# S4 of the split weights made by an addition on POOL instead of an accumulating transfer, and the first addition of a pair issued 8 units ahead

## The chip, the cores and the metric

The kernel runs on one core of one Trainium2 chip. The metric is the device time of one execution in microseconds (us). TensorE (PE) multiplies, VectorE (DVE) and ScalarE (ACT) prepare weights and activations, GpSimd (POOL) here issues transfers that add into on-chip memory (SBUF) and does a few elementwise operations, and SyncE (SP) issues the plain transfers.

## The reference

One layer of a hybrid encoder for 512 tokens with 1024 features, in float32: a half-step SwiGLU feed-forward network (ffn1), a mixer (a chunked state-space scan beside chunked attention), a second half-step feed-forward network (ffn2), and a final norm. The change touches the two feed-forward networks alone:

```python
def swiglu(h, w_gate, w_up, w_down):
    return (jax.nn.silu(h @ w_gate) * (h @ w_up)) @ w_down

x = x + 0.5 * swiglu(rms_norm(x, ffn1_norm[i]), ffn1_w_gate[i], ffn1_w_up[i], ffn1_w_down[i])
...
x = x + 0.5 * swiglu(rms_norm(x, ffn2_norm[i]), ffn2_w_gate[i], ffn2_w_up[i], ffn2_w_down[i])
```

The hidden width is 2816.

## The kernel before, in words

**Products.** Most of the feed-forward work uses Winograd's form of the 2x2 block product, with seven products in place of eight. For a piece d of the gate and up weights (128x1024 floats in each of its four blocks A11, A12, A21, A22) the stationary operands are P1: A11, P2: A12, P4: A22, P5: S1 = A21 + A22, P6: S2 = S1 + A11, P3: S4 = S2 + A12, and P7: A11 + A21. The sign conventions of the stored blocks make every one of these a sum. One product of one piece is a *unit* of 24 matmuls of 128x128 by 128x256 (line 541). The pieces of the first stretch of a network are multiplied plainly (units A11 to A22).

**The sums.** S1, S2 and S4 are built in place, in one tile per piece, `view(d)` (rows show it as `s`; there are four such places, in two wide tiles). A plain SP transfer brings A21 (line 324), and then POOL issues three transfers of 512 KB that add what they bring to what is there (`more`, line 327): A22 for P5, A11 for P6, A12 for P3. The single blocks g (P1), g2 (P2) and u2 (P4) come by SP into a `raw` tile (line 320, four buffers); P7's sum is added into g's buffer by POOL in the same way.

**Splits.** Float32 operands are multiplied as a rounded part and a remainder. `usplit` makes both for one weight tile: ACT casts (line 272) and DVE subtracts (line 274), into one of four rotating `xw` slots. `ws.get()` hands out the parts of the current unit and first makes the splits of the units up to 3 ahead. A transfer is issued when its unit is no more than its *lead* ahead: the numbers 14, 10, 6 and 5 in `product`. A step that reuses a tile waits for the split that last read it.

**Order.** Nothing is scheduled by a planner: each engine works through its instructions in the order in which the code emits them, and waits on semaphores. From the second Winograd piece on, a network runs P5(d), P1(d), P3(d-1), P4(d-1), P6(d), P2(d), P7(d). P6 and P7 are copied out of PSUM by ACT (lines 546 and 549); the two halves of the network's activations are then combined and split on DVE and ACT (lines 464, 465, 483 to 490, 522 to 570).

**The down projection** is cut into three blocks of pieces, named by tuples (n, a); the first two blocks are done in Winograd form in both networks (the third in ffn2 alone, with an order of its own, written out). A block takes its pieces in pairs: `down()` runs one product of both pieces, for token half t = 0 and then t = 1, 12 matmuls of 128x512 each (lines 142 to 144), and DVE adds each finished PSUM bank to the residual x at once (line 610). Products P1, P6, P7, P3 and P4 in turn go on accumulating in the banks of P1 (`X`) or in their own (`H`, `L`): P6 adds onto P1's banks, so its matmuls of a half wait until DVE has read P1's half. `DOWN` is the order of the products.

Of the kernel before, what the change touches and what calls it, by code (L numbers as in the profile page):

```python
# [12 lines left out]
ALU = mybir.AluOpType  # L13
# [24 lines left out]
def hybrid_block(ctx: ExitStack, tc, xT, xt, par, wgu1, wd1, ws1, win, wdt, wv, wo, rbt, wgu2, ws2, fin, out):  # L38
    nc = tc.nc
    V, S, G, T = nc.vector, nc.scalar, nc.gpsimd, nc.tensor  # L40
# [4 lines left out]
    def sb(tag, shape, dt=F32, bufs=1):  # L45
        uid[0] += 1
        return pool.tile(shape, dt, tag=tag, name=f"{tag}_{uid[0]}", bufs=bufs)
# [9 lines left out]
    def f(ap):  # L57
        return ap.bitcast(F32)
# [51 lines left out]
    class Stream:  # L110
# [16 lines left out]
        def get(self):  # L127
            i = self.used
            self.used += 1
            while self.done < min(len(self.jobs), i + 1 + self.look):  # L130
                job = self.jobs[self.done]
                job.move(0, True)
                job.parts = job.split()
                self.done += 1
            for n in range(self.done, min(len(self.jobs), i + 18)):
                self.jobs[n].move(n - i)
            return self.jobs[i].parts
# [95 lines left out]
    def wide_tile(g, dt=F32R):  # L233
        if g not in wide or wide[g][0] != dt:
            wide[g] = dt, sb(f"s{g}", [P, GROUPS[g], SEQ], dt)
        return wide[g][1]
# [30 lines left out]
    def usplit(src):  # L267

        i = turn[0] % 4
        turn[0] += 1  # L270
        hi = sb(f"xw{2 * i}", list(src.shape), F32R)
        S.copy(out=hi, in_=src)  # L272
        lo = sb(f"xw{2 * i + 1}", list(src.shape), F32R)
        V.tensor_tensor(out=lo, in0=src, in1=f(hi), op=ALU.subtract)  # L274
        return hi, lo

    DOWN = ("P5", "P1", "P2", "P6", "P7", "P3", "P4")

    def program(plain, by_tokens):


        if plain == 1:
            out = [("A11", 0), ("A21", 0), ("A12", 0), ("P1", 1), ("P5", 1), ("A22", 0), ("P6", 1), ("P2", 1), ("P7", 1)]
        else:
            out = [(a, d) for d in range(plain) for a in ("A11", "A21", "A12", "A22")]
            out += [(p, plain) for p in ("P5", "P1", "P6", "P2", "P7")]
        out = [("P", p, d) for p, d in out]
        for d in range(plain + 1, ND):  # L290
            out += [("P", p, e) for p, e in (("P5", d), ("P1", d), ("P3", d - 1), ("P4", d - 1), ("P6", d), ("P2", d),
                                             ("P7", d))]
            for n in range(2):
                if d == BLOCKS[n][1]:
                    out += [("S", n, p, (0, 1)) for p in DOWN]
        last = [("P", p, ND - 1) for p in ("P3", "P4")]
        if by_tokens == 3:
            return out + last + [("S", 2, p, (c,)) for c in range(2) for p in ("P5", "P1") + ("P2",) * (c == 0)] + [
                ("S", 2, "P6", (0, 1)), ("S", 2, "P2", (1,))] + [("S", 2, p, (0, 1)) for p in ("P7", "P3", "P4")]
        out += [("D", 2, 0, 0)] + last + [("D", 2, 1, 0), ("D", 2, 0, 1), ("D", 2, 1, 1)]  # L300
        return out + [("D", 2, o, c) for o in range(2, KD) for c in range(2)]

    def ffn_weights(wgu, plain, by_tokens, wst, wd=None):


        bufs, jobs, views = {}, {}, []

        def view(d):
            if d not in bufs:
                i = views.index(d)  # L310
                m = 2 if type(d) is int else min(2, BLOCKS[d[0]][1] - d[1])
                bufs[d] = wide_tile((40, 52)[i // 2 % 2], F32)[:, 2 * (i % 2):2 * (i % 2) + m]
                if type(d) is int:
                    bufs[d] = bufs[d].rearrange("p a (k c) -> p a k c", c=P)
            return bufs[d]

        def whole(key, src):
            def go():
                bufs[key] = sb("raw", list(src.shape), bufs=4)
                nc.sync.dma_start(out=bufs[key], in_=src)  # L320
            return go

        def first(d, src):
            return lambda: nc.sync.dma_start(out=view(d), in_=src)

        def more(get, src):
            return lambda: G.dma_start(out=get(), in_=src, accum_op=ALU.add)  # L327

        def product(p, d, A):

            sum_ = lambda: view(d)
            raw = {"P1": "g", "P2": "g2", "P4": "u2"}.get(p)
            if p[0] == "A":
                n = ("A11", "A12", "A21", "A22").index(p)
                j = Job(lambda: usplit(bufs[p, d]), (6, "raw", whole((p, d), A[n])))
            elif raw:
                j = Job(lambda: usplit(bufs[raw, d]), (6 if p == "P1" else 5, "raw",
                                                       whole((raw, d), A[("P1", "P2", "", "P4").index(p)])))
            elif p == "P5":
                views.append(d)  # L340
                before = jobs["P3", views[-5]] if len(views) > 4 else None
                j = Job(lambda: usplit(view(d)), (14, before, first(d, A[2])), (10, None, more(sum_, A[3])))
            elif p == "P6":
                j = Job(lambda: usplit(view(d)), (6, jobs["P5", d], more(sum_, A[0])))
            elif p == "P7":
                j = Job(lambda: usplit(bufs["g", d]), (6, jobs["P1", d], more(lambda: bufs["g", d], A[2])))
            else:
                j = Job(lambda: usplit(view(d)), (6, jobs["P6", d], more(sum_, A[1])))
            jobs[p, d] = j
            if p == "P7":  # L350
                jobs["P1", d].holds = j
            ws.jobs.append(j)

        for step in program(plain, by_tokens):
            if step[0] == "P":
                p, d = step[1:]
                product(p, d, wgu[d])
            elif step[0] == "S":
                n, p, pieces = step[1:]
                for a in [BLOCKS[n][0] + 2 * c for c in pieces]:  # L360
                    product(p, (n, a), [wst[i, :, a:min(a + 2, BLOCKS[n][1]), :] for i in range(4)])
            else:
                n, o, c = step[1:]
                if c == 0:
                    a, b = 2 * BLOCKS[n][0], 2 * BLOCKS[n][1]
                    ws.add(wd[o, :, a:b, :], b - a, P)
                    late = ws.jobs.pop() if (n, o) in ((2, 0), (2, 1)) else None
                    if late:
                        jobs["late", o] = late
                elif ("late", o) in jobs and n == 2:  # L370
                    ws.jobs.append(jobs["late", o])

    class XCombos:
# [40 lines left out]
        def split(self, d, src):  # L414
            S.copy(out=d[0], in_=src)
            V.tensor_tensor(out=d[1], in0=src, in1=f(d[0]), op=ALU.subtract)
# [25 lines left out]
    def ffn(xc, n_plain, early, by_tokens, rc, between, after):  # L442
# [174 lines left out]
        for step in program(n_plain, by_tokens):  # L617
            if step[0] == "S":
# [4 lines left out]
                down(*step[1:])  # L623
                past = step[1:3] == (1, DOWN[-1])
                continue
# [786 lines left out]
```

## Time and profile before

| what | value |
|---|---|
| median of 3 runs | 1033.45 us (1032.77 to 1034.1) |
| profiled execution, its own time | 1034.42 us |
| span of its instructions | 1032.6 us |
| mean granted TensorE clock | 0.995 of full speed |
| PE busy | 1007.5 us, 98% of the span |
| DVE, ACT, POOL busy | 809.0, 587.9, 162.2 us |

The profile is of one execution. Its own time is 1.82 us longer than the span, which begins with the first and ends with the last instruction, and 0.97 us above the median of the three timed runs. An engine's busy time is the sum over its instructions; a stall of PE shows as idle time before one of its rows, with what ended it.

### The profile page before, as it was taken

How to read it: one execution, taken by the hardware profiler on the slowest of the kernel's cores; microseconds unless marked ns; L12 is line 12 of the kernel's file. 1: busy time of each engine (PE TensorE's matmuls, PEld its weight loads, DVE VectorE, ACT ScalarE, POOL GpSimd, SP SyncE). 2: the span in 40 equal slices, each digit the busy share in tenths (PEclk: the TensorE clock that was granted, in tenths of full speed). 3: DMA queues.
4: the chain of work that ended last, by engine and by line, in shares of the span. 5: the costliest groups of instructions: out<-in, count | busy, mean ns of one | idle time of the engine just before them, and what ended most of it. 6: DMA issues, size and time to landing. Idle time of an engine off the chain costs nothing.

```text
span 1032.6 us, 16130 instructions
## 1 busy us (share of the span) xinstructions
PE 1007.5 (98%) x6154; PEld 888.0 (86%) x6154; DVE 809.0 (78%) x1351; ACT 587.9 (57%) x929; POOL 162.2 (16%) x185
## 2 busy tenths in 40 slices
PE   9999999999999999999999999999999999999985
PEld 7899889998998777777878778879998899989974
DVE  7878767886676697978867999797687678867876
ACT  7556445653564456646656876656654356534535
POOL 1111112121120013323201011101212121212110
PEclk9999999999999999999999999999999999999998
DMA  9979888996753322222232223765888989989672
GB/s 317 291 156 236 181 231 185 227 205 160 195 117 97 102 82 62 66 78 68 67 100 74 82 83 103 227 140 124 193 201 188 236 198 229 202 194 206 154 143 81
DMA packets 47933, 162.14 MB, mean 157 GB/s; under 512 B 5232, under 2 KB 6000, under 8 KB 47856
## 3 DMA queue, kind: packets, MB, share of 16 engines
q0 software_dynamic: 16704, 59.78, 33.2%
q1 hardware_dynamic: 28272, 95.43, 27.3%
q10 hardware_dynamic: 2880, 5.91, 1.7%
q8 instruction: 48, 0.79, 0.3%
q14 instruction: 29, 0.24, 0.1%
HBM read 159.00 MB, written 2.10 MB: 156 GB/s over the span
## 4 chain that ended last, share of the span: by engine, by line
PE 80%; DVE 9%; issue 4%; DMA 4%; ACT 3%; POOL 0%; SPq 0%; ACTq 0%; DVEq 0%; POOLq 0%
PE mm L541 19%; PE aux L541 14%; PE mm L142 10%; PE mm L143 10%; PE mm L144 10%; PE aux L144 3%; PE aux L143 3%; PE aux L142 3%; DMA raw<-wgu 2%; DVE fs L829 2%; DMA s<-wgu 1%; DVE wlo L86 1%; DVE xw L274 1%; ACT xw L272 1%; PE aux L953 1%
## 5 line engine op out<-in xcount | busy, mean ns | idle before, releaser
L541 PE MATMUL mm<-s,xw 128*128 128x256 f32 x1824 | 229.2, 283 | 2.8 <-ACT fu L549 2.8
L541 PEld LDWEIGHTS mm<-s,xw 128*128 128x128 f32 x1824 | 222.2, 191 | 4.1 <-ACT fu L549 3.4
L272 ACT CAST xw<-raw 128x1024 fp32r<-128x1024 f32 (+1 forms) x127 | 131.3, 1036 | 150.1 <-PE mm L541 54.6
L274 DVE TENSOR_TENSOR xw<-raw,xw 128x1024 fp32r<-128x1024 f32 (+1 forms) x127 | 152.7, 1203 | 63.8 <-ACT xw L272 63.7
L541 PE MATMUL aux<-s,xw 128*128 128x256 f32 x1368 | 174.1, 283 | 0.0
L541 PEld LDWEIGHTS aux<-s,xw 128*128 128x128 f32 x1368 | 168.8, 192 | 0.6
L272 ACT CAST xw<-s 128x1024 fp32r<-128x1024 f32 (+1 forms) x87 | 90.0, 1035 | 118.7 <-PE mm L144 40.1
L142 PE MATMUL mm<-xw,whi 128*128 128x512 f32 x364 | 149.6, 411 | 0.0
L274 DVE TENSOR_TENSOR xw<-s,xw 128x1024 fp32r<-128x1024 f32 (+1 forms) x87 | 104.7, 1203 | 56.9 <-ACT xw L272 55.0
L143 PE MATMUL mm<-xw,whi 128*128 128x512 f32 x364 | 144.8, 398 | 0.0
L144 PE MATMUL mm<-xw,wlo 128*128 128x512 f32 x364 | 144.4, 397 | 0.0
L84 ACT CAST whi<-raw 128x512 fp32r<-128x512 f32 (+1 forms) x104 | 62.2, 601 | 66.1 <-PE mm L143 46.9
L327 POOL DMA_DIRECT2D s<-wgu x57 | 51.4, 940 | 307.7 <-DMA s<-wgu 139.7
L86 DVE TENSOR_TENSOR wlo<-raw,whi 128x512 fp32r<-128x512 f32 (+1 forms) x104 | 74.3, 715 | 13.9 <-ACT whi L84 13.4
L142 PEld LDWEIGHTS mm<-xw,whi 128*128 128x128 f32 x364 | 68.9, 189 | 16.5 <-issue 2.2
L143 PEld LDWEIGHTS mm<-xw,whi 128*128 128x128 f32 x364 | 68.8, 189 | 16.2 <-issue 1.2
L144 PEld LDWEIGHTS mm<-xw,wlo 128*128 128x128 f32 x364 | 68.7, 189 | 16.2
L327 POOL DMA_DIRECT2D s<-ws x30 | 26.1, 869 | 167.9 <-DVE xw L274 70.2
L143 PE MATMUL aux<-xw,s 128*128 128x512 f32 x106 | 42.1, 397 | 2.9 <-DVE xw L274 2.9
L144 PE MATMUL aux<-xw,s 128*128 128x512 f32 x106 | 42.2, 398 | 0.0
L142 PE MATMUL aux<-xw,s 128*128 128x512 f32 x106 | 41.6, 394 | 0.0
L884 POOL TENSOR_TENSOR fu<-dt,tri 128x512 fp32r<-128x512 f32 x16 | 18.9, 1189 | 95.9 <-PE aux L935 45.5
(297 smaller groups left out, 1745.8 us busy)
## 6 DMA issues: line engine op xcount, KB each, us to landing
raw<-wgu SPq DMA_DIRECT2D x68, 512.0 KB, 5.6
s<-wgu POOLq DMA_DIRECT2D x57, 512.0 KB, 6.2
raw<-win SPq DMA_DIRECT2D x28, 512.0 KB, 3.5
s<-ws POOLq DMA_DIRECT2D x27, 512.0 KB, 5.7
raw<-ws SPq DMA_DIRECT2D x27, 512.0 KB, 4.6
s<-wgu SPq DMA_DIRECT2D x19, 512.0 KB, 5.4
raw<-wgu POOLq DMA_DIRECT2D x19, 512.0 KB, 5.8
raw<-wo SPq DMA_DIRECT2D x12, 512.0 KB, 3.7
```

Of the source, the lines that this page charges most:

```text
L84: S.copy(out=hi, in_=src)
L86: V.tensor_tensor(out=lo, in0=src, in1=f(hi), op=ALU.subtract)
L142: T.matmul(ps, lhsT=sh, rhs=mh, start=start, stop=False, skip_group_check=skip)
L143: T.matmul(ps, lhsT=sh, rhs=ml, start=False, stop=False, skip_group_check=skip)
L144: T.matmul(ps, lhsT=sl, rhs=mh, start=False, stop=stop, skip_group_check=skip)
L272: S.copy(out=hi, in_=src)
L274: V.tensor_tensor(out=lo, in0=src, in1=f(hi), op=ALU.subtract)
L327: return lambda: G.dma_start(out=get(), in_=src, accum_op=ALU.add)
L541: T.matmul(ps[:, j * HS:(j + 1) * HS], lhsT=sw[:, j, k], rhs=m, start=(p in ("P1", "P2", "P5") and j == 0 and k == 0 and n == 0), stop=(k ...
L829: V.scalar_tensor_tensor(out=y[:, d:SEQ], in0=u[:, 0:SEQ - d], scalar=cw(j), in1=y[:, d:SEQ], op0=ALU.mult, op1=ALU.add)
L884: G.tensor_tensor(out=r, in0=f(src[:, c, h0:h0 + 4]).unsqueeze(2).broadcast_to([P, 4, P]), in1=tri.unsqueeze(1).broadcast_to([P, 4, P]), o ...
L953: T.matmul(py[HD * (h % 2):HD * (h % 2) + HD, (h // 2) * P:(h // 2 + 1) * P], lhsT=xd[:, h * HD:(h + 1) * HD], rhs=st["m"][h // 4][:, (h % ...
```

## The change

For the pieces of the gate and up weights, and for blocks 0 and 1 of the down projection, P3's job has no transfer any more. The split of P2 first emits one POOL addition, `view(d) = view(d) + g2`, 128x1024 floats, and then its own cast and subtraction; A12 is the block g2, which P2 has in SBUF. The addition reads `view(d)` after P6's split has read it (S2 is in it until then) and reads the g2 buffer, so the next transfer into that buffer waits for it too. In `DOWN` P6 moves ahead of P2, so that S2 has been split when P2's split emits the addition. The lead of P5's second transfer goes from 10 to 8. Block 2 of ffn2's down projection keeps the transfer.

```diff
-    DOWN = ("P5", "P1", "P2", "P6", "P7", "P3", "P4")
+    DOWN = ("P5", "P1", "P6", "P2", "P7", "P3", "P4")
...
             sum_ = lambda: view(d)
+            here = type(d) is int or d[0] < 2
             raw = {"P1": "g", "P2": "g2", "P4": "u2"}.get(p)
...
+            elif p == "P2" and here:
+                def split():
+
+                    G.tensor_tensor(out=view(d), in0=view(d), in1=bufs[raw, d], op=ALU.add)
+                    return usplit(bufs[raw, d])
+                j = Job(split, (5, "raw", whole((raw, d), A[1])))
...
-                j = Job(lambda: usplit(view(d)), (14, before, first(d, A[2])), (10, None, more(sum_, A[3])))
+                j = Job(lambda: usplit(view(d)), (14, before, first(d, A[2])), (8, None, more(sum_, A[3])))
...
+            elif here:
+                j = Job(lambda: usplit(view(d)))
             else:
                 j = Job(lambda: usplit(view(d)), (6, jobs["P6", d], more(sum_, A[1])))
```

POOL's queue around the first down block and the first pieces after it, in ffn1. `s_45` and `s_113` are the two wide tiles of sums, `raw` the single blocks, `ws` the down weights and `wgu` the gate and up weights. Before (P6 of the block's first two pieces, P7, S4 of both, then the second additions of P5(4) on, with S4 of piece 5 the row 33):

```order
23 L327 DMA s_113_472<-ws 128x1024
24 L327 DMA s_45_150<-ws 128x1024
25 L327 DMA raw_1094<-ws 128x1024
26 L327 DMA raw_1132<-ws 128x1024
27 L327 DMA s_113_472<-ws 128x1024
28 L327 DMA s_45_150<-ws 128x1024
29 L327 DMA s_113_472<-wgu 128x1024
30 L327 DMA s_45_150<-wgu 128x1024 x2
31 L327 DMA raw_1394<-wgu 128x1024
32 L327 DMA s_113_472<-wgu 128x1024
33 L327 DMA s_45_150<-wgu 128x1024
```

And of the change, the same stretch:

```order
24 L327 DMA s_113_472<-ws 128x1024
25 L327 DMA s_45_150<-ws 128x1024
26 L327 DMA raw_1095<-ws 128x1024
27 L327 DMA raw_1133<-ws 128x1024
28 L340 TENSOR_TENSOR s_113_472<-s_113_472,raw_1244 128x1024
29 L340 TENSOR_TENSOR s_45_150<-s_45_150,raw_1276 128x1024
30 L327 DMA s_113_472<-wgu 128x1024
31 L327 DMA s_45_150<-wgu 128x1024 x2
32 L327 DMA raw_1395<-wgu 128x1024
33 L327 DMA s_113_472<-wgu 128x1024
34 L340 TENSOR_TENSOR s_45_150<-s_45_150,raw_1506 128x1024
```

Each S4 transfer is replaced in its place by an addition, and no other row of POOL moves: also the second addition of P5 stands where it stood, with a lead of 8 as with 10. There are 27 such rows in the kernel.

DVE's queue in the same down block: the residual additions (line 610 before, 619 after) of P5 (`aux`) and P1 (`mm`), and between them the remainders (line 274) of the next products. Before:

```order
144 L610 SCALAR_TENSOR_TENSOR x_62<-aux_1234,rcf_312,x_62 128x4x128
145 L274 TENSOR_TENSOR xw_220_1275<-raw_1201,xw_219_1273 128x1024
146 L610 SCALAR_TENSOR_TENSOR x_62<-aux_1235,rcf_312,x_62 128x4x128
147 L274 TENSOR_TENSOR xw_222_1280<-raw_1238,xw_221_1278 128x1024
148 L610 SCALAR_TENSOR_TENSOR x_62<-mm_1236,rcf_312,x_62 128x4x128
149 L274 TENSOR_TENSOR xw_226_1313<-s_113_472,xw_225_1311 128x1024
150 L610 SCALAR_TENSOR_TENSOR x_62<-mm_1237,rcf_312,x_62 128x4x128
151 L274 TENSOR_TENSOR xw_228_1319<-s_45_150,xw_227_1317 128x1024
152 L610 SCALAR_TENSOR_TENSOR x_62<-aux_1309,rcf_312,x_62 128x4x128
```

After:

```order
144 L619 SCALAR_TENSOR_TENSOR x_62<-aux_1235,rcf_312,x_62 128x4x128
145 L274 TENSOR_TENSOR xw_219_1274<-s_113_472,xw_218_1272 128x1024
146 L619 SCALAR_TENSOR_TENSOR x_62<-aux_1236,rcf_312,x_62 128x4x128
147 L274 TENSOR_TENSOR xw_222_1281<-s_45_150,xw_221_1279 128x1024
148 L619 SCALAR_TENSOR_TENSOR x_62<-mm_1237,rcf_312,x_62 128x4x128
149 L274 TENSOR_TENSOR xw_224_1313<-raw_1244,xw_223_1311 128x1024
150 L619 SCALAR_TENSOR_TENSOR x_62<-mm_1238,rcf_312,x_62 128x4x128
151 L274 TENSOR_TENSOR xw_226_1318<-raw_1276,xw_225_1316 128x1024
152 L619 SCALAR_TENSOR_TENSOR x_62<-mm_1237,rcf_312,x_62 128x4x128
```

P6's two remainders (from `s`) now stand at the places of P2's (from `raw`), and PE's 24 matmuls of P6 likewise ahead of P2's: the product that follows P1 is the one that goes on in P1's banks (`mm_1237`, `mm_1238`). This happens in four blocks, two in each network. On PE, ACT, DVE and SP nothing else changes its place.

## Rows read from the trace of the kernel before

**Rows 1.** The page's sections 1 and 3: busy time, transfer queues.

```profile
PE 1007.5 (98%) x6154; PEld 888.0 (86%) x6154; DVE 809.0 (78%) x1351; ACT 587.9 (57%) x929; POOL 162.2 (16%) x185
...
q0 software_dynamic: 16704, 59.78, 33.2%
```

**Rows 2.** What PE waited for: us in total, times, longest us.

```profile
PE mm L541 <- ACT fu L549: 2.8, 2, 2.1
```

**Rows 3.** Timeline of PE and ACT, ffn1 near P7(5): start, us, instruction [idle].

```profile
166.44 0.74 PE L541 MATMUL mm<-s,xw 128*128 128x256 f32 x4 [2.06 <-ACT fu L549]
...
162.47 1.05 ACT L272 CAST xw<-s 128x1024 fp32r<-128x1024 f32 x1 [4.55 <-DMA s<-wgu]
...
165.81 0.57 ACT L549 COPY fu<-mm 128x512 f32<-128x512 f32 x1
```

**Rows 4.** Timeline of PE and ACT, ffn2, the same place.

```profile
838.43 1.33 PE L541 MATMUL mm<-s,xw 128*128 128x256 f32 x9 [0.71 <-ACT fu L549]
...
834.46 1.05 ACT L272 CAST xw<-s 128x1024 fp32r<-128x1024 f32 x1 [3.20 <-DMA s<-wgu]
```

**Rows 5.** Line 327's transfers issued at 154.83, 827.74 and 165.18, in this order.

```profile
DMA to landing us min/median/max: 7.5/7.5/7.5
...
DMA to landing us min/median/max: 6.6/6.6/6.6
...
DMA to landing us min/median/max: 5.3/5.3/5.3
```

**Rows 6.** Timeline of SP's queue from 154: two transfers in one row.

```profile
155.17 3.58 SPq L320 DMA_DIRECT2D raw<-wgu  x2
```

**Rows 7.** Timeline of POOL in the mixer: additions of two inputs, 128x512.

```profile
400.56 1.04 POOL L884 TENSOR_TENSOR fh<-dt,tri 128x512 fp32r<-128x512 f32 x1
401.56 1.04 POOL L884 TENSOR_TENSOR fu<-dt,tri 128x512 fp32r<-128x512 f32 x1
...
413.09 1.48 POOL L884 TENSOR_TENSOR fh<-dt,tri 128x512 fp32r<-128x512 f32 x1
```

**Rows 8.** Timeline of DVE beside the last two of those.

```profile
413.60 0.27 DVE L958 TENSOR_TENSOR s<-s,aux 128x128 f32<-128x128 f32 x1
413.80 1.33 DVE L86 TENSOR_TENSOR wlo<-raw,whi 128x512 fp32r<-128x512 f32 x1
415.05 1.00 DVE L918 COPY dt<-s 128x4 f32<-128x4 f32 x1
```

**Rows 9.** Line 918 over the kernel: ns min/median/max, first and last start.

```profile
L918 DVE COPY dt<-s x12: 153/556/1017, 401.9 to 501.2; 128x4 f32<-128x4 f32 x12
```

**Rows 10.** Timeline of DVE, ACT and PE in ffn1 after P6(2)'s split.

```profile
51.71 1.23 DVE L274 TENSOR_TENSOR xw<-s,xw 128x1024 fp32r<-128x1024 f32 x1 [2.81 <-ACT xw L272]
...
53.45 0.68 DVE L465 TENSOR_TENSOR wlo<-fa,whi 128x512 fp32r<-128x512 f32 x1
...
59.82 0.58 ACT L546 COPY fa<-mm 128x512 f32<-128x512 f32 x1
...
60.45 1.81 PE L541 MATMUL mm<-s,xw 128*128 128x256 f32 x13
```

**Rows 11.** Timeline of DVE, PE and POOL in ffn2 after P6(1)'s split.

```profile
697.94 1.23 DVE L274 TENSOR_TENSOR xw<-s,xw 128x1024 fp32r<-128x1024 f32 x1 [0.59 <-ACT xw L272]
...
699.97 0.68 DVE L198 TENSOR_TENSOR s<-ident,rq_h 128x512 fp32r<-128x512 f32 x1
...
700.80 0.47 PE L205 MATMUL aux<-s,onesr 128*128 128x512 f32 x1 [0.18 <-DVE s L198]
...
699.58 0.86 POOL L327 DMA_DIRECT2D s<-wgu  x1 [9.96 <-DVE rq_r L171]
```

**Rows 12.** Timeline of DVE and PE in ffn1's first down block.

```profile
113.58 1.23 DVE L274 TENSOR_TENSOR xw<-raw,xw 128x1024 fp32r<-128x1024 f32 x1 [1.77 <-ACT xw L272]
...
120.27 0.74 DVE L610 SCALAR_TENSOR_TENSOR x<-mm,rcf,x 128x512 f32<-128x512 f32 x1
...
121.94 0.39 PE L142 MATMUL aux<-xw,s 128*128 128x512 f32 x1
```

## The prediction

> **What bounds the kernel now.** The page's first section says that PE is busy for 1007.5 of 1032.6 us [rows 1]. So a change to the weights' preparation can only give back PE's few stalls or make new ones, and the view to read next is that of PE's waits. Of its entries the two networks' weight path owns one that this change can reach: P7's first matmuls waiting for ACT's copy of P6 out of PSUM, 2.8 us in two places [rows 2]. The timeline shows both. In ffn1 PE stood still for 2.06 us ahead of P7(5), because the copy stood in ACT's queue behind the cast of P5(6), and that cast waited 4.55 us for a transfer; in ffn2 the same place cost 0.71 us, and there the cast waited 3.20 us [rows 3, 4]. Everywhere else in the Winograd stretches PE runs on from unit to unit, so transfers and splits are hidden there, and 27 fewer transfers on a queue that is 33.2% busy [rows 1] are worth nothing in themselves. What the change is worth is read at those two places, and at the places where the new additions stand in DVE's way.
>
> **What it removes: two late landings.** P5(6)'s second transfer was issued at 154.83 and took 7.5 us to land; its like in ffn2, issued at 827.74, took 6.6; one that runs alone takes 5.3 [rows 5]. What came between is in SP's queue: 0.34 us after the issue SP started a plain transfer of 512 KB [rows 6], P4(5)'s block into the buffer that P2(5)'s split had just given up. With the change that buffer is also read by the addition for piece 5, and that addition stands on POOL right behind P5(6)'s transfer (rows 33 and 34 of the order above). So SP's transfer can't start until POOL has issued, waited and added, some 3 us later, and P5(6)'s transfer goes first. At 5.3 us it lands 2.2 us earlier in ffn1 and 1.3 us earlier in ffn2. Both are more than the stall, so I take back all of both: **-2.06 and -0.71, together -2.8 us**. P4(5) is used two units after P5(6)'s split is cast and has the time to be late by 3 us. The bound on the other side is nothing at all, if the transfers still share the engines in a way that leaves P5(6) late; that is a rival below.
>
> **What it removes at no gain.** The other S4 transfers land unwaited for. The lead of 8 in place of 10 moves no row in any queue; nothing is counted for it. The stall in ffn2's last block, which keeps the transfer, stays as it is.
>
> **What one addition costs.** No row of before is a 128x1024 addition on POOL. The nearest are POOL's products of two inputs at 128x512 in the mixer: 1.04 us each with starts 1.00 apart when nothing disturbs them [rows 7]. Twice that is **a = 2.04 us**, and that is the value I take. Below it can't be under 1.04, the price of half the elements. Above, the same operation took 1.48 us in a stretch where DVE worked beside it [rows 7], so 2.96 for the double size; but that figure has DVE's turns in it, so I put the upper end midway, at 2.5.
>
> [...]
>
> **What it does to DVE.** POOL itself has the time (162 us busy [rows 1], and 27 additions bring 55). The question is whether DVE runs beside it. In the mixer it didn't, for operations that read SBUF: next to POOL's products a DVE copy of 4 elements took 1.00 us, where the shortest of the same line took 0.153, and a 128x512 remainder 1.33, while an operation with an operand in PSUM kept its 0.27 [rows 8, 9]. Each engine's instruction waited for the other's to end. So I take an addition as a time a in which DVE's remainders, splits and small operations stand still, and its readings of PSUM don't.
>
> The addition starts as soon as P6's remainder has ended on DVE, that is where DVE has just come back to its backlog. In most units there is slack for that: the splits run up to 3 units of 2.9 us ahead, and ACT's copy of P6 usually ends a good microsecond before P7. I found three kinds of places without it.
>
> *ffn1, piece 2.* P6(2)'s remainder ends at 52.94. The addition then holds DVE to about 55.05, and the activations' remainder that began at 53.45 begins there, 1.6 us late. It is the head of a chain through DVE (lines 483, 484) and two casts on ACT to ACT's copy of P1 at 59.82, which ended at 60.40, when PE began the next unit at 60.45 [rows 10]. There is no slack at the end and 0.1 to 0.2 on the way: **+1.4 us**.
>
> *ffn2, piece 1.* The remainder ends at 699.17. What follows on DVE is the chain of small operations that makes the norm's scale for PE: its last one ran from 699.97 and PE waited for it already, 0.18 us, before 700.80 [rows 11]. The addition falls into this chain (the transfer that it replaces was issued at 699.58 [rows 11]) and delays its end by all of a: **+2.0 us**. If DVE's row gets in first, the next one is caught, so I see no way past it short of the addition starting after 699.97.
>
> *The down blocks.* Here the swapped order matters. P6 now follows P1 and adds onto P1's banks, so PE needs DVE's reading of P1's second half when P6's second half begins. In the first block that is at 121.94, and without additions DVE would be done by 120.27 + 0.74 = 121.01 [rows 12]: 0.9 us to spare. With them DVE's row is: first remainder of P6 until 113.58 + 1.23 = 114.81; first addition from 114.90; second remainder of P6 until 116.13 + a; second addition from 116.22 + a; P2's remainder, which stands ahead of the reading, until 117.45 + 2a; the reading until 118.10 + 2a (rows of DVE overlap by 0.09). With a = 2.04 that is 122.18, a stall of 0.24; below a = 1.92 there is none. Four such blocks: **+1.0 us**, and this is the term that hangs most on a: 8 us for each us of it.
>
> **The sum.** -2.8 + 1.4 + 2.0 + 1.0 = +1.6 us. On the profiled execution's 1034.42 that is 1036.0; that execution was 0.97 us above the median, so against the median of 1033.45 the forecast is **1035.1 us**, 0.16% slower. A difference under 0.2%, 2.07 us here, is about what a measurement of this kernel can't tell from no change. The sum moves by 10 us for each us of a (two single places and eight times in the blocks), so a = 2.08 would already pass that limit, and with a = 1.92 the sum is +0.4.
>
> **The rivals.**
>
> *DVE is not held up.* If a contiguous addition leaves DVE its operands, all three losses vanish and the gain of 2.8 stays: 1030.7 us, faster. For it speaks that every unit has slack for one slower remainder, and that the slowed rows are all from one stretch of the mixer; against it that those rows show nearly whole waits, not a mild stretching. An addition as short as 1.04 us would hold DVE so little that the blocks cost nothing and the two places 0.4 and 1.0: 1032.1, no change that can be told. Chance of a faster result 0.2.
>
> *The addition is dearer.* With a from 2.1 to 2.5 the blocks decide: midway, at 2.3, each stalls by 0.76, and the sum is -2.8 + 1.7 + 2.3 + 3.0 = +4.2, which gives 1037.6; at 2.5 it is +6.2 and 1039.7. For it speaks that two separate inputs at full length have no row here; against it the 1.04. Chance 0.26. [...]
>
> *P5(6) stays late.* If its transfer doesn't come earlier (the late landing being due to something other than SP's transfer, or the addition finding its operands early enough to be issued first), the gain is gone and the sum is 1.4 + 2.0 + 1.0 = +4.4: 1037.9, slower. The issue at 155.17 right behind that at 154.83 speaks against it. Chance 0.12.
>
> **How the numbers follow.** My own case, losses and gain nearly level, has 0.42, and its own range is 1033.9 to 1035.5 (a from 1.92 to 2.08). The two slower rivals together have 0.38, the faster one 0.2. For eight times in ten the range reaches down to 1031.0, just above the case in which DVE isn't held at all, and up to 1038.2, past a = 2.3 and past a late P5(6), and short of a = 2.5.
>
> **What would show it.** In the trace of the changed kernel: additions of about 2.04 us at line 340, 27 of them. P7(5) without idle time ahead of it in both networks, P5(6)'s transfers landing in about 5.3 us, SP's transfer behind POOL's addition. A new wait of about 1.4 us of PE ahead of ffn1's unit near 60.4 (for ACT's line 555), one of 2 us at line 205 in ffn2 near 701, and waits at line 142 for DVE's line 619 of 0.2 us in each of four blocks. DVE's remainders beside an addition should show more than 1.23 us or begin as it ends. I am wrong if DVE's rows run at their usual length beside the additions, if the addition takes clearly other than 2 us, or if a unit that I took to have slack stalls.

## The result and the profile after

The changed kernel takes 1041.49 us (median of 8 runs, 1039.33 to 1042.15), the kernel before 1033.78 us on the same chip. The ratio is 1.0068, with a 95% interval of 1.0053 to 1.0084: some 7 us slower (the two medians stand 7.7 us apart), outside the forecast range of 1031.0 to 1038.2. The profiled execution took 1040.57 us, 6.15 us more than that of before, so it holds most of the difference.

The page's section 1 of the changed kernel, to be read beside [rows 1]:

```profile
PE 1010.3 (97%) x6154; PEld 888.5 (86%) x6154; DVE 848.5 (82%) x1351; ACT 590.0 (57%) x929; POOL 205.1 (20%) x185
...
q0 software_dynamic: 12816, 45.62, 25.2%
```

POOL's queue lost 14 MB, as intended, and POOL gained 43 us of work. The telling number is DVE's: 39.5 us more busy time with the same 1351 instructions. Part of that is waiting: a remainder of DVE that POOL held up is recorded as busy for 2.99 us (at 116.51, below), where one in [rows 10] took 1.23.

What PE waited for, to be read beside [rows 2] (us in total, times, longest us):

```profile
PE aux L143 <- DVE xw L274: 3.4, 1, 3.4
PE aux L205 <- DVE s L198: 2.4, 1, 2.4
PE mm L142 <- DVE x L619: 1.8, 4, 0.5
...
PE mm L550 <- ACT fa L555: 1.2, 1, 1.2
...
PE mm L550 <- ACT fu L558: 0.2, 1, 0.2
```

All three predicted waits are there and the one that was to go has gone (ACT's copy, line 558 now, from 2.8 us to 0.2). The first row is ffn2's last block, which the change leaves alone; it waited 2.9 us before.

The groups of POOL (busy us, mean ns of one):

```profile
L340 POOL TENSOR_TENSOR s<-s,raw 128x1024 f32<-128x1024 f32 x27 | 69.3, 2567 | 39.8 <-DVE xw L274 30.1 <-DVE rq_q L169 9.7
```

and line 340 by itself (ns min/median/max):

```profile
L340 POOL TENSOR_TENSOR s<-s,raw x27: 2377/2413/2793, 52.4 to 971.7; 128x1024 f32<-128x1024 f32 x27
```

An addition takes 2.41 us, and none took less than 2.377. I had put a = 2.04.

**Where the 6 us went.** Both kernels run the same 6154 matmuls in the same order but for the four swapped pairs, so the start of each can be compared with that of the same number before. The lag of the changed kernel grows and shrinks in few places: +1.2 us at ffn1's piece 2, +3.7 at ffn2's piece 1, 0.8 to 0.9 in each of the four blocks (3.4), -2.3 and -1.0 at the two P7(5), +0.5 near 206 us, +0.6 in ffn2's last block, and nothing in sum over the rest. Together 6.1. Each trace is of one execution: the first 58 us, ahead of the first loss, moved by -0.6 to +1.1 us from trace to trace, so a lag of half a us in one place is proof of nothing by itself.

At ffn2's piece 1 (timeline of DVE, POOL and PE, beside [rows 11]):

```profile
700.22 0.15 DVE L169 TENSOR_TENSOR rq_q<-rq_o 128x4 f32<-128x4 f32 x1
700.41 2.38 DVE L171 SCALAR_TENSOR_TENSOR rq_r<-rq_q,rq_v 128x4 f32<-128x4 f32 x1
702.82 0.16 DVE L173 SCALAR_TENSOR_TENSOR rq_o<-rq_r,rq_o 128x4 f32<-128x4 f32 x1
...
700.39 2.38 POOL L340 TENSOR_TENSOR s<-s,raw 128x1024 f32<-128x1024 f32 x1 [9.69 <-DVE rq_q L169]
...
704.14 0.77 PE L205 MATMUL aux<-s,onesr 128*128 128x512 f32 x1 [2.39 <-DVE s L198]
```

The addition started 0.02 us ahead of an operation on 4 elements, which then lasted as long as the addition, 2.38 us in place of 0.16. The norm's chain is late by all of it, and PE stood still for 2.39 us. What I had not counted follows (windows of PE: start and end, busy us, granted clock, DMA share):

```profile
700.00:704.00 4.00, 1.75 (x12) 1.00 0.00 0
704.00:705.00 1.00, 0.86 (x3) 0.57 0.00 0
705.00:706.00 1.00, 1.00 (x6) 0.50 0.00 0
706.00:707.00 1.00, 1.00 (x6) 0.50 0.46 33
707.00:708.00 1.00, 1.00 (x9) 0.73 0.55 197
708.00:709.00 1.00, 1.00 (x11) 1.00 0.72 295
```

Behind the idle time the granted clock was 0.50 of full speed for some 3 us; the lag grew by another 1.5 us there.

In ffn1's first block (timeline of DVE, POOL and PE, beside [rows 12]):

```profile
116.51 2.99 DVE L274 TENSOR_TENSOR xw<-s,xw 128x1024 fp32r<-128x1024 f32 x1
119.42 0.74 DVE L619 SCALAR_TENSOR_TENSOR x<-mm,rcf,x 128x512 f32<-128x512 f32 x1
120.26 2.82 DVE L274 TENSOR_TENSOR xw<-raw,xw 128x1024 fp32r<-128x1024 f32 x1
123.00 0.74 DVE L619 SCALAR_TENSOR_TENSOR x<-mm,rcf,x 128x512 f32<-128x512 f32 x1
...
116.02 2.40 POOL L340 TENSOR_TENSOR s<-s,raw 128x1024 f32<-128x1024 f32 x1 [2.03 <-DVE xw L274]
119.58 2.41 POOL L340 TENSOR_TENSOR s<-s,raw 128x1024 f32<-128x1024 f32 x1 [1.17 <-DVE xw L274]
...
123.80 0.50 PE L142 MATMUL mm<-xw,whi 128*128 128x512 f32 x1 [0.46 <-DVE x L619]
```

This is the row that the prediction laid out: remainder, addition, remainder, addition, P2's remainder, and only then the reading of P1's second bank, which PE waits for. The remainders start in time and end 1.1 us after the addition does (119.50 after 118.42, 123.08 after 121.99). The reading itself, an operand in PSUM, keeps its 0.74, also beside the second addition.

### The profile page after: what moved, and what is told of

Its sections match the earlier page's. It is cut to its first block, busy times and chain, and to the rows that moved or that the text cites. A ratio compares the mean times of both kernels' runs of the same rounds, so it can differ in the third digit from the quotient of the medians.

```text
span 1038.8 us, 16095 instructions
## 1 busy us (share of the span) xinstructions
PE 1010.3 (97%) x6154; PEld 888.5 (86%) x6154; DVE 848.5 (82%) x1351; ACT 590.0 (57%) x929; POOL 205.1 (20%) x185
## 4 chain that ended last, share of the span: by engine, by line
PE 81%; DVE 9%; ACT 3%; issue 3%; DMA 2%; POOL 0%; SPq 0%; ACTq 0%; POOLq 0%; DVEq 0%
PE mm L550 20%; PE aux L550 15%; PE mm L142 10%; PE mm L143 10%; PE mm L144 10%; PE aux L144 3%; PE aux L143 3%; PE aux L142 3%; DVE fs L838 2%; DVE xw L274 1%; DMA raw<-wgu 1%; ACT xw L272 1%; DVE wlo L86 1%; PE aux L962 1%; PE aux L753 1%
## 5 line engine op out<-in xcount | busy, mean ns | idle before, releaser
L274 DVE TENSOR_TENSOR xw<-raw,xw 128x1024 fp32r<-128x1024 f32 (+1 forms) x127 | 180.8, 1425 | 50.6 <-ACT xw L272 50.2
L274 DVE TENSOR_TENSOR xw<-s,xw 128x1024 fp32r<-128x1024 f32 (+1 forms) x87 | 111.7, 1284 | 44.4 <-ACT xw L272 44.0
L327 POOL DMA_DIRECT2D s<-wgu x38 | 33.4, 880 | 278.7 <-DMA s<-wgu 152.8
L340 POOL TENSOR_TENSOR s<-s,raw 128x1024 f32<-128x1024 f32 x27 | 69.3, 2567 | 39.8 <-DVE xw L274 30.1
L327 POOL DMA_DIRECT2D s<-ws x22 | 19.2, 874 | 123.8 <-DMA s<-ws 58.7
```

Of the source, the lines that this page charges most:

```text
L340: G.tensor_tensor(out=view(d), in0=view(d), in1=bufs[raw, d], op=ALU.add)
```

## The experiments

The diffs are against the changed kernel unless they say otherwise. The ratios are to the kernel before, with 95% intervals.

**1. Additions in the blocks alone** (`blocks_only`).

```diff
-            here = type(d) is int or d[0] < 2
+            here = type(d) is tuple and d[0] < 2
```

> Additions in the four down blocks alone, with the swapped order; all pieces of the gate and up weights keep the transfer. Theory (DVE stands still for 2.41 us per addition, and the reading of P1's second bank behind two of them makes PE wait): about +0.8 us per block over before, together +3.3 us (1.003), a wait of PE at line 142 for line 619 of about 0.5 us in each block; the late landings of P5(6) stay, 2.2 and 0.9 us. Rival (the blocks are harmless and the pieces carry the whole loss): no difference from before.

Measured: 1.0035 (1.0021 to 1.0049), +3.6 us. PE's waits for line 619 are the same four, 1.8 us in all; the lag grows by 0.8 to 0.9 us in each block. The theory holds and its rival falls: eight of 27 additions make half of the loss.

**2. Additions for the gate and up pieces alone** (`pieces_only`): `here = type(d) is int`, and the old `DOWN`.

> Additions for the gate and up pieces alone; the blocks keep transfer and old order. Theory: +1.2 (ffn1 piece 2), +3.7 (ffn2 piece 1, with the half clock behind the stall), +0.4 (piece 7), -3.1 (P5(6)): +2.2 us over before (1.002), 3.5 us under the whole change. Rival (blocks harmless): as slow as the whole change, +6 to +7 us.

Measured: 1.0035 (1.0020 to 1.0050), +3.6 us, a little over the 2.2 expected and with the interval's low end below it. The trace has the same waits (2.4 us at line 205, 1.0 for line 555) and none for line 619 in the blocks.

**3. The same without the first Winograd piece of each network** (`pieces_not_first`): `here = type(d) is int and d > plain`, and the old `DOWN`.

> As the pieces alone, but the first Winograd piece of each network (2 in ffn1, 1 in ffn2) keeps the transfer too. Theory: both single places are gone and the gain of 3.1 us at P5(6) stays: 2 to 3 us faster than before (0.9975). Rival (the gain at P5(6) comes with a loss that is spread over all units): no faster than before.

Measured: 0.9987 (0.9973 to 1.0002), 1.3 us faster, less than expected and not clear of no change, so the time alone doesn't rule the rival out. Against run 2 the medians differ by 4.7 us (1037.81 and 1033.07), which is about what the two places cost by the lags (1.2 + 3.7). The wait for line 555 is gone and that at line 205 is back at 0.2 us. The gain at P5(6) is in the lags (-2.3 and -1.0), and 0.8 us are lost again behind three remainders that were held up for longer than a unit's slack ("What was not foreseen", below).

**4. The addition on VectorE** (`on_dve`): `V.tensor_tensor` in place of `G.tensor_tensor`.

> The whole change with the addition on VectorE instead of POOL, at about 1.2 us. Theory (what costs is the time in which DVE does nothing else): the blocks lose nothing (two times 1.2 is under the 3.85 us of room), ffn2 piece 1 loses 1.2 us and perhaps the clock, ffn1 piece 2 nearly nothing, P5(6) is still relieved as SP's transfer waits 1.2 us more: between 2 us faster than before and no difference, and 6 us or more faster than the change. Rival (the loss comes from S4 made in SBUF or from the new order as such): as slow as the change.

Measured: 1.0017 (1.0002 to 1.0032), 1.8 us slower than before and 5 us faster than the change. The addition takes 1.22 us on DVE, and no block waits. Two things came out otherwise than I expected. Line 205 had no wait at all: the program put five more matmuls ahead of it on PE, so this place is no test (and PE's order is not only that in which the code is written, though the part on the kernel before says so). And P5(6) stayed late, with 3.6 us of waits ahead of the two P7(5):

```profile
PE mm L550 <- ACT fu L558: 3.6, 2, 1.9
```

The timeline of POOL and SP and, below it, the landing of line 327 issued at 155.62 say why:

```profile
155.62 0.86 POOL L327 DMA_DIRECT2D s<-wgu  x1 [9.45 <-DMA s<-wgu]
...
155.89 3.44 SPq L320 DMA_DIRECT2D raw<-wgu  x2
```

```profile
DMA to landing us min/median/max: 7.2/7.2/7.2
```

On DVE the addition is done before P2's remainder, so nothing holds SP's transfer back; it starts 0.27 us after POOL's and that one lands late, as in [rows 5, 6]. By the lags the two P7(5) cost 1.0 us each more than before, which comes to the loss of this run; at the first of them it is the clock, at 0.50 for some 3 us behind the wait.

This run also settles a rival that the prediction didn't name. Before, POOL issued the transfer of S4 of piece 5 right behind that of P5(6), two in one row:

```profile
154.83 1.77 POOL L327 DMA_DIRECT2D s<-wgu  x2 [9.24 <-DMA s<-wgu]
```

Here that second transfer is gone, SP's isn't held back, and P5(6)'s still takes 7.2 us. So it is SP's transfer that makes it late, and not that of S4.

**5. The swapped order and the lead alone** (`swap_lead_only`): `here = False`.

> No additions at all: only P6 ahead of P2 in the blocks, and the lead of 8. Theory: no difference from before (under 0.1%), since DVE would read P1's second bank 0.9 us before P6 needs it. Rival (the swapped order itself makes PE wait): +1 to +3 us, with waits at line 142 for line 619.

Measured: 1.0007 (0.9987 to 1.0028), no difference that can be told, and no wait for line 619. The order as such costs nothing in the blocks of this trace; it only takes away the slack that the additions then overdraw.

**6. One addition per network, for piece 5** (`piece5_only`): `here = d == 5`, and the old `DOWN`.

> One addition per network, for piece 5; everything else as before (the lead of 8 apart). Theory: SP's transfer now waits for that addition, P5(6)'s transfer lands in 5.1 to 5.4 us, and the stalls of 2.06 and 0.71 us ahead of P7(5) are gone: 2.8 to 3.1 us faster than before (0.997). Rival (the relief came from the other transfers that were removed): no difference.

Measured: 0.9976 (0.9958 to 0.9994), 2.5 us faster than before and the lowest ratio here, though its interval overlaps those of runs 3 and 9. Timeline of POOL, SP and PE, and below it the landing of line 327 issued at 154.91:

```profile
154.91 0.86 POOL L327 DMA_DIRECT2D s<-wgu  x1 [9.47 <-DMA s<-wgu]
155.47 2.74 POOL L340 TENSOR_TENSOR s<-s,raw 128x1024 f32<-128x1024 f32 x1
...
158.24 2.02 SPq L320 DMA_DIRECT2D raw<-wgu  x2
...
164.44 0.74 PE L550 MATMUL mm<-s,xw 128*128 128x256 f32 x4 [0.21 <-ACT fu L558]
```

```profile
DMA to landing us min/median/max: 5.5/5.5/5.5
```

SP's transfer waits until 158.24, P5(6)'s lands in 5.5 us where it took 7.5, and 2.06 us of PE's idle time become 0.21. With 25 of the 27 transfers back in place, the gain is all there: with run 4, where 27 transfers are gone and the gain is missing, it is a matter of who goes first, not of fewer bytes.

**7. Each addition in two halves** (`halves`): a loop over the two 128x512 parts of `view(d)` and g2.

> The whole change, but each addition as two of 128x512. Theory (a DVE instruction waits for the POOL instruction in progress to end, and they take turns): a half takes about 1.25 us; in ffn2 piece 1 the small operation waits 1.2 us, the next one for the second half, so the chain is about as late as before (2 to 2.4 us); in the blocks DVE's remainder gets in between the halves, with no or little gain in all: within 2 us of the change. Rival (DVE slips in freely at each boundary and is done after one half): waits at line 205 and in the blocks halved, 3 us or more faster than the change.

Measured: 1.0035 (1.0020 to 1.0051), 3.4 us faster than the change, more than the theory allowed. Here theory and rival were each right in a place. At ffn2's piece 1 (timeline of DVE and POOL):

```profile
699.50 1.29 DVE L171 SCALAR_TENSOR_TENSOR rq_r<-rq_q,rq_v 128x4 f32<-128x4 f32 x1
700.82 1.19 DVE L173 SCALAR_TENSOR_TENSOR rq_o<-rq_r,rq_o 128x4 f32<-128x4 f32 x1
702.05 0.17 DVE L194 CAST rq_h<-rq_o 128x4 fp32r<-128x4 f32 x1
...
699.48 2.52 POOL L342 TENSOR_TENSOR s<-s,raw 128x512 f32<-128x512 f32 x2 [9.65 <-DVE rq_q L169]
```

One small operation waits for each half, so PE still stood still for 2.3 us. In the blocks a remainder of DVE goes between the halves (in the first block remainders last 1.88, 1.63 and 1.65 us, where the change had 2.99 and 2.82), each is a whole instruction's worth of work, and the reading of P1's bank comes in time: no wait for it is left. In these places turns are taken by whole instructions. They aren't everywhere: some remainders waited for both halves, and the two longest, at 75.90 and 891.70 (4.25 and 4.34 us), cost 0.6 us each by the lags. With ffn2's piece 1 (3.7) and the gain at P5(6) (-3.1) that is 1.8 of this execution's 3.2 us of lag; another 1.1 arose in the first 10 us, ahead of any addition.

**8. What an addition costs by its inputs** (`price`), against the kernel before: five operations on POOL ahead of the attention stage.

```diff
+    G.tensor_tensor(out=pr, in0=x[:, 0:2], in1=x[:, 2:4], op=ALU.add)
+    G.tensor_tensor(out=pr[:, 0], in0=x[:, 0], in1=x[:, 2], op=ALU.add)
+    G.tensor_tensor(out=pr[:, 0], in0=x[:, 0], in1=x[:, 2], op=ALU.mult)
+    G.tensor_tensor(out=p4(pr[:, 0]), in0=wide4, in1=p4(x[:, 2]), op=ALU.add)
+    G.tensor_tensor(out=p4(pr[:, 0]), in0=wide4, in1=ones.unsqueeze(1).broadcast_to([P, 4, P]), op=ALU.mult)
```

> The kernel before with five extra POOL operations ahead of the attention stage, whose results nothing uses: an addition 128x1024, an addition 128x512, a product 128x512, an addition 128x512 with one input that repeats 4 values, a product 128x512 with both inputs repeated. Theory (the price depends on how the inputs are read): the first about 2.4 us, the full 128x512 ones about 1.2, the repeated ones about 1.04 as line 884. Rival (a price per element plus a fixed one, whatever the inputs): all 128x512 alike at 1.04 and the first at 2.4 for another reason.

The first and the last of the five are its lines 1244 and 1248. These two rows and, from run 7, that of line 342 (ns min/median/max):

```profile
L1244 POOL TENSOR_TENSOR raw<-x x1: 2392/2392/2392, 544.1 to 544.1; 128x1024 f32<-128x1024 f32 x1
...
L1248 POOL TENSOR_TENSOR raw<-x,ones x1: 1041/1041/1041, 555.2 to 555.2; 128x512 f32<-128x512 f32 x1
```

```profile
L342 POOL TENSOR_TENSOR s<-s,raw x54: 1259/1606/2292, 53.1 to 971.2; 128x512 f32<-128x512 f32 x54
```

With both inputs repeated from fewer values (line 884 reads its inputs like that, 4 values spread over 128 each and a 128x128 tile repeated) 512 elements take 1.04 us; with both read in full they take 1.26 at the least. The three operations between had DVE's turns in them (timeline of POOL: addition, product, addition with one repeated input; below it the instruction of DVE that each waited for):

```profile
548.38 1.80 POOL L1245 TENSOR_TENSOR raw<-x 128x512 f32<-128x512 f32 x1
...
550.26 1.63 POOL L1246 TENSOR_TENSOR raw<-x 128x512 f32<-128x512 f32 x1
...
553.76 1.31 POOL L1247 TENSOR_TENSOR raw<-x 128x512 f32<-128x512 f32 x1
```

```profile
548.34 0.69 DVE L86 TENSOR_TENSOR wlo<-raw,whi 128x512 fp32r<-128x512 f32 x1
...
549.55 1.19 DVE L86 TENSOR_TENSOR wlo<-raw,whi 128x512 fp32r<-128x512 f32 x1
...
553.48 0.69 DVE L86 TENSOR_TENSOR wlo<-raw,whi 128x512 fp32r<-128x512 f32 x1
```

Counted from the end of DVE's instruction, the addition and the product of full inputs both needed 1.15 us (550.18 - 549.03, 551.89 - 550.74), and the addition with one repeated input 0.90 (555.07 - 554.17), as line 884's products do before where DVE held them up (0.89 to 0.90 for the four that began from 411.57 to 415.99). The halves of run 7 need 1.15 there as well. So in these rows it is the repeated input that is cheaper and one is enough (shown by one row), and addition or product makes no difference.

**9. The change without its losses** (`harmless`): `here = d > plain if type(d) is int else d[0] < 2`, with two halves in the blocks alone.

> The change with its two kinds of loss taken out by their causes: the first Winograd piece of each network keeps the transfer, and each addition of the blocks is made as two of 128x512, so that DVE gets in between. 25 of the 27 transfers are still gone. Theory: no wait at line 205 beyond 0.2 us, none for line 555, none in the blocks, and the 3 us at P5(6) are gained: 1 to 2.5 us faster than before (0.998 to 0.999), 8 us or more faster than the change. Rival (part of the loss belongs to the additions as such): slower than before.

Measured: 0.9989 (0.9968 to 1.0010), not to be told from before (the 1 to 2.5 us of gain aren't shown), and about 8 us faster than the change, with 25 of its 27 additions. None of the three waits is left beyond what before had, and the gain at P5(6) shows in the lags (-2.3 and -1.0 us); 0.3 us each near 206 and 898 us, a longer wait in the last block (3.2 us, before 2.9) and the clock behind it (0.50 for some 5 us, before for some 3) take part of it back.

**10. One addition in the whole kernel, at ffn2's piece 1** (`ffn2_first_only`): `here = plain == 1 and d == 1`, and the old `DOWN`.

> One addition in the whole kernel, for ffn2's piece 1; all else as before, the lead of 8 apart. Theory: PE waits 2.2 us longer at line 205 and then runs at half clock for about 3 us, which costs another 1.5 us: +3.7 us (1.0036). Rival (the half clock in the other traces was chance): +2.2 us (1.002), with the granted clock at 1.00 behind the wait.

Measured: 1.0044 (1.0023 to 1.0066), +4.5 us. The interval has my number and just leaves out the rival's, but in the one execution that was profiled it went as the rival says. Windows of PE behind the wait of 2.39 us, which ended at 703.79:

```profile
704.00:705.00 1.00, 1.00 (x8) 1.00 0.00 0
705.00:706.00 1.00, 1.00 (x11) 1.00 0.00 0
```

The granted clock stayed at 1.00, and the lag grew by 2.2 us. The rest of this execution's delay of 5.6 us lies elsewhere, 0.7 us of it in the first 10 us, ahead of the addition. The largest part, 2.6 us, is at ffn2's P7(5): PE waited there for 1.76 us, 1.0 more than before, and behind that wait the granted clock fell to 0.50 for some 3 us. So the half clock came in this kernel too, in another place. Whether it came at piece 1 in the other executions isn't on record.

## Why the prediction was wrong

**The step that failed: the price of one addition.** The prediction took a = 2.04 as twice a row of 1.04 [rows 7]. The measured price is 2.41. The row was not of the same kind: it is a product (the heading of [rows 7] calls it an addition) whose inputs repeat, and reading two full inputs costs 1.26 per 512 elements (run 7) and 2.39 per 1024 (run 8). The prediction said that the sum moves by 10 us for each us of a; 0.37 us more moves it from +1.6 to +5.3, and the median from 1035.1 to 1038.8, past the upper end of the range. The rival "the addition is dearer" was the case that came, and nearly at its upper end of 2.5; the measured median lies above even the 1039.7 that it gives there. What was weighed against it, that one row, was a weak argument. A slip in the sum besides: by its own terms a = 2.08 gives +2.0, just under the limit of 2.07 and not past it.

**The blocks** (+1.0) were mis-sized by that step alone. With a = 2.41 the working of the prediction gives a reading that ends at 122.92, a wait of 0.98; measured are 0.8 to 0.9 us per block, 3.4 in all. Runs 1 and 5 show that it is the additions in the new order, and not the order.

**ffn2's piece 1** (+2.0): the mechanism was right and the wait 2.2 us longer. What was missing is the clock behind it, at 0.50 for some 3 us in the changed kernel and in runs 2 and 7, which cost 1.5 us more, but at 1.00 in run 10 behind the same wait. So this part is a risk of such a wait and no fixed price.

**ffn1's piece 2** (+1.4): measured 1.2.

**P5(6)** (-2.8): measured -2.3 and -1.0. Runs 4 and 6 show the cause: SP's transfer, which goes beside POOL's unless an addition holds its buffer. Over the kept traces P5(6)'s transfer landed in 6.4 to 7.5 us wherever SP's began between 0.3 us before and 0.8 us after it, and in 5.3 to 5.5 wherever an addition on POOL held SP's to 3.3 us or more behind. In ffn2 the stall can also stay away by itself: in run 5, with no addition, SP's began 0.9 us behind, POOL's landed in 5.7, and the lag there was -1.0 too. So the gain in ffn1 is the additions'; the one in ffn2, in one trace against one, isn't shown to be theirs.

**DVE is held up**: right. The rival that it isn't is out: 4 elements took 2.38 us beside an addition and 0.16 before. In run 7 two small operations took 1.29 and 1.19 us, one for each half: each lasted until a whole instruction of POOL had ended. What in the chip makes one engine wait for the other, no trace shows.

**What was not foreseen**: +0.5 near 206 us, where one of ffn1's remainders lasted 4.15 us. The timeline of DVE and POOL, and below it the same remainder before, with what POOL did beside it:

```profile
196.10 4.15 DVE L274 TENSOR_TENSOR xw<-raw,xw 128x1024 fp32r<-128x1024 f32 x1 [1.65 <-ACT xw L272]
...
195.84 0.88 POOL L327 DMA_DIRECT2D s<-ws  x1 [7.16 <-DMA s<-ws]
196.40 2.75 POOL L340 TENSOR_TENSOR s<-s,raw 128x1024 f32<-128x1024 f32 x1
```

```profile
196.49 1.23 DVE L274 TENSOR_TENSOR xw<-raw,xw 128x1024 fp32r<-128x1024 f32 x1 [1.65 <-ACT xw L272]
...
195.62 1.19 POOL L327 DMA_DIRECT2D s<-wgu  x1
```

I took the units in between to have slack for one addition. Most had. This remainder began while POOL was issuing a transfer with the addition right behind it, and the addition went first. The issue by itself held nothing up: before, the remainder began inside one too and took 1.23 us. In the traces of the changed kernel and of runs 2, 3, 7 and 9 there are 26 remainders that began so or just as the issue ended. Of these, 24 waited for the addition and lasted 3.5 to 4.3 us; the two that began within 0.1 us of the issue's start went first. Why is open. What such a wait costs shows in PE's lag some 10 us later: less than 0.1 us up to 3.75, 0.14 at 3.82, 0.45 at 4.15, 0.65 at 4.34. So this chain has room for a remainder 2.5 us longer than its 1.2, and what goes beyond is paid in full.

The 0.6 in the last block can't be put down to the change: that block's lag moved by -0.6 to +1.5 us in the other traces, most in run 6, which has two additions.

With a = 2.41 the prediction's sum is +5.3, where the trace has +6.1. The rest is what the terms above missed in both directions, the clock's 1.5 us the largest.

## What to carry to other kernels

Work moved to POOL was paid here by DVE where both read SBUF: beside additions of 2.4 us a remainder of 1.23 lasted 2.99 and an operation on 4 elements 2.38 in place of 0.16 (in [rows 8] a copy was held up too), while a reading of PSUM kept its 0.74. So count each elementwise instruction of POOL as time in which such work of DVE stands still, and look for the places where DVE's queue feeds the engine that bounds the kernel with less slack than one such instruction (or two in a row, or one with the rest of a transfer's issue). If it must be there, cut it into pieces that are shorter than that slack (in the blocks the halves left none of the 1.8 us of waits) and leave the critical chains alone (at ffn2's piece 1 they left 2.3 us of 2.4). For a price, look for a row with the same shape and the same way of reading its inputs (512 elements took 1.04 us here with repeated inputs and 1.26 at the least in full); when the sum has a slope of 10 us per us, a rough price doesn't carry a forecast of 1 us.

A transfer that lands late may need no fewer bytes, only a later start of the one that is issued just behind it (here 3.33 us behind in place of 0.34, and 5.5 us to landing in place of 7.5): two additions of the 27 brought the whole gain here.

## What the runs showed of the hardware

A DVE instruction that POOL holds up is recorded as busy for the whole wait (2.99 us for a remainder that takes 1.23 elsewhere), so DVE's share rose from 78% to 82% with the same 1351 instructions. After a wait of 2.39 us with PE idle, the granted clock fell to 0.50 for 3 us in the changed kernel, and stayed at 1.00 in run 10 behind a wait of the same length at the same place; in run 10 it fell behind a wait of 1.76 us elsewhere, and before it stayed at 1.00 behind the 2.06 us of [rows 3]. So the length of the wait alone doesn't tell; what decides it stays open. On POOL 512 elements of two full float32 inputs took 1.26 us at the least and of repeated ones 1.04.
